# Merging the convolution branch last: two branch merges taken out of the attention's filler steps, and fewer filler steps per turn

## The chip, the cores and the metric

The kernel runs on one core of a Trainium2 chip. The metric is device time in microseconds (us) for one execution of the whole program. The engines are PE (TensorE, matrix products and transposes), DVE (VectorE), ACT (ScalarE), POOL (GpSimd) and SP (SyncE, which issues most of the DMAs). Each of them works through its own list of instructions strictly in the order in which the list was built; semaphores make one engine wait for another.

## The reference

Two layers of a decoder trunk over 512 tokens of 1024 channels, in f32. In each layer three token mixers read the same normalised input `h`, each is projected to 1024 channels by its own matrix, and the three are added under per-channel gates:

```python
h = rmsnorm(x, norm_mix[layer])
z = h @ w_in[layer]
u_glu, q_nsa, kv_nsa, g_nsa, c_q, c_kv, k_rope, g_merge = jnp.split(z, split_at, axis=-1)
y_conv = conformer_conv(u_glu, ...)          # GLU, 31 taps per channel, layernorm, swish, @ w_branch_conv
y_nsa = nsa_attention(q_nsa, ...) @ w_branch_nsa[layer]
y_mla = mla_attention(c_q, c_kv, ...) @ w_branch_mla[layer]
g_conv, g_attn, g_mla = jnp.split(jax.nn.sigmoid(g_merge), 3, axis=-1)
x = x + (g_conv * y_conv + g_attn * y_nsa + g_mla * y_mla) @ w_out[layer]
```

Cross attention over 256 memory tokens and a gated feed-forward net follow in each layer, and one last norm at the end.

## The kernel before, in words

**Arithmetic.** An f32 operand is held as two fp32r parts, a high and a low one. `hilo` (L90) makes them: ACT copies the high part (L93), DVE subtracts it for the low part (L94). A product of two such operands is three matmuls (`mm3`, L85 to L88). One such triple with 512 columns is called a *step* here. Weights come by DMA into `raw` (2 buffers of 1 MB), and `unit` (L105) splits them into `wh` and `wl` (3 buffers each), one unit for 8 steps.

**One layer's mixers** are built by `mix` (L453). The main line of work there is attention, unit by unit: four heads of the latent attention (MLA), then the sparse attention (NSA) in the order of two groups `g`, in each four query tiles `i` = 3, 2, 1, 0 and for each a compressed unit and the selected and window branches (two units of two heads each for `i` > 1, one of four heads otherwise). A unit has scores on PE (`ps_s`, L1020 and L1021), a biased minimum on DVE (L1025), the exponential on ACT (L1028), a reciprocal and gate product on DVE (L1033, L1034), the scaling on ACT (L1036), transposes on PE (`ps_t`, L1065), the split of the transposed probabilities (`PTh` on ACT, `PTl` on DVE) and the products with the values on PE (`ps_pv`, L1075 and L1076). `ps_s`, `ps_t`, `PTh` and `PTl` have two buffers each, `ps_pv` has one. When a query tile is done, `mixture` (L1082) copies and adds it into `o_nsa` (ACT L1088, DVE L1092), and only then has the next tile's `ps_pv` a bank.

**The filler.** Between the attention's instructions stand steps that do not depend on them. `work` (L1095) is a generator of all of these, in one fixed order: the projections and compressions that NSA needs, the convolution's four channel blocks, and at its end two of the three branch merges. `pump(n)` takes the next n steps from it. The loop over the units calls `pump` once per turn (transpose, scores of a later unit, products):

```python
for now in mix(*args, ready[u]):
    next(scores, None)
    products()
    products = now
    pump(6 if u < 4 else 4 if args[1] > 1 else 3)
```

Here `u < 4` are the MLA heads and `args[1]` is the query tile `i`. After the loop `run(filler)` takes what is left, and the third merge, that of NSA, follows.

**The convolution.** `conv_steps(m)` (L553) takes 16 steps on PE, then one DVE instruction at L567 and 30 at L569 (`ca<-u,vT,ca`, one for each tap, called *taps* here). The taps are given a low priority: the builder places them in DVE's list where it finds room. The layer norm and swish are eight jobs: `conv_stats(t)` transposes one token tile on PE (L878, into a `ps_mm` bank), takes mean and variance on DVE (L881 to L883), a power on POOL (L884), and writes `cn` on DVE (L886), which frees the bank; `conv_swish(m)` transposes back (L896), then ACT and DVE make `cS`.

**A merge** (`merge_steps(b, w, act)`, L916) handles one branch b (0 convolution, 1 NSA, 2 MLA) in 8 blocks of 128 channels. Each block has 8 gate steps, which need only `h` (`hTh`, `hTl`), and 4 steps with the branch's output `act` (`om` for MLA, `op` for the two others); so 96 steps in all. The gate of block m + 1 comes ahead of block m's own 4 steps. Branch 2 starts the sum `acc` (L946), the others add to it (L948, L949), and the last one makes `fin`, the split operand of the output projection. The `ps_mm` tag has 3 banks, shared by gates, blocks and the convolution's jobs.

**What sets the order.** The builder keeps, for each engine, roughly the order in which the code is written, but moves an instruction ahead where what stands before it is not ready by its own reckoning. The list that comes out is fixed; the chip follows it.

Of the kernel before, what the change touches and what calls it, by code (L numbers as in the profile page):

```python
# [21 lines left out]
NT = T // 128  # L22
# [30 lines left out]
def kernel(ctx, tc, x, mem, positions, rel_bias, norm_mix, norm_xattn, norm_mem, norm_ffn, norm_final,  # L53
# [399 lines left out]
    def mix(l, x_src, g_mix, x_now, more_x, spill_x, turns):  # L453
# [356 lines left out]
        o_mla = []  # L810
# [62 lines left out]
        cS = []  # L873
# [42 lines left out]
        def merge_steps(b, w, act):  # L916
            blocks = fm_blocks(W, [Z_M + b * D + 128 * m for m in range(KD)], KD)

            def gate():
                p = bank("mm")  # L920
                yield from fm_steps(p, next(blocks), hx, KD)
                gt = new("gm")
                nc.scalar.activation(gt, p, AF.Tanh, scale=0.5)
                ahead.append(gt)

            ahead = []
            yield from gate()
            for m in range(KD):
                if m + 1 < KD:
                    yield from gate()  # L930
                if m % 4 == 0:
                    raw = load(lambda raw: [(raw.rearrange("p (k c) -> p k c", k=4),
                                             w[:, m * 128:m * 128 + 512].rearrange("(k p) c -> p k c", p=128))])
                    rv = raw.rearrange("p (k c) -> p k c", k=4)
                if m % 2 == 0:
                    c = m % 4 * 128
                    wh, wl = unit(rv[:, :, c:c + 256], (4, 256))
                e = m % 2 * 128
                y = bank("mm")
                for k in range(4):  # L940
                    yield
                    mm3(y, wh[:, k, e:e + 128], wl[:, k, e:e + 128], act[k][0], act[k][1], k == 0, k == 3)
                gt = ahead.pop(0)
                if b == 2:
                    acc.append(new("op", name="acc"))
                    nc.vector.scalar_tensor_tensor(acc[m], gt, 1.0, y, op0=OP.add, op1=OP.mult)  # L946
                    continue
                nc.vector.scalar_tensor_tensor(gt, gt, 1.0, y, op0=OP.add, op1=OP.mult)  # L948
                nc.vector.tensor_tensor(acc[m], acc[m], gt, op=OP.add)  # L949
                if b == 1:  # L950
                    fin.append((new("op", dt=F32R), new("op", dt=F32R)))
                    hilo(fin[m][0], fin[m][1], acc[m], 0.5)

# [141 lines left out]
        def work():  # L1095
# [22 lines left out]
            next(out_v)  # L1118
            done.update(("values", "group 1"))
            yield from third  # L1120
            yield from conv_steps(3)

            jobs = {84 + 3 * t: (conv_stats, t) for t in range(NT)} | {99 + 3 * m: (conv_swish, m) for m in range(4)}
            for n, _ in enumerate(chain(merge_steps(2, w_branch_mla[l], o_mla), merge_steps(0, w_branch_conv[l], cS))):
                if n in jobs:
                    yield
                    job, i = jobs[n]
                    job(i)
                yield


        idle = cycle(("s", "t", "s", "t", "pv"))
# [73 lines left out]
        for u, (_, mix, args) in enumerate(units):  # L1206
            scores = start(u + 2 if u < 3 else u + 3)
            for now in mix(*args, ready[u]):
                next(scores, None)
                products()  # L1210
                products = now
                pump(6 if u < 4 else 4 if args[1] > 1 else 3)
            for _ in scores:
                pump(1)
        products()
# [2 lines left out]


        paced["rate"] = 0.17  # L1220
        run(merge_steps(1, w_branch_nsa[l], split4([o_nsa[0][:, k, :] for k in range(4)])))
        return fin, vT[:, 173:181]

    def raw_halves():
# [570 lines left out]
```

## Time and profile before

| | |
|---|---|
| median of 3 runs | 1900.68 us (1900.39 to 1902.31) |
| the profiled execution | 1901.39 us |
| span of its trace | 1899.7 us |
| PE busy | 1877.8 us, 99% of the span |
| DVE busy | 1509.5 us, 79% |
| ACT busy | 1042.1 us, 55% |

All rows are of the one profiled execution; a place in the program is given by its time in us from the span's start. In layer 0 the sparse attention runs from about 190 to 421, and the last merge from there to about 486; layer 1 repeats this some 937 later. In a row of a group, "x12 | 14.7, 1221 | 8.0 <-ACT wh L93" means 12 instructions, 14.7 us busy, 1221 ns for one, and 8.0 us in which the engine stood idle just before them, most of it until that ACT instruction. A matmul's printed length covers its pipeline; what one costs PE is the distance between two starts.

### The profile page before, as it was taken

What the parts mean: (1) busy time and instruction counts of PE and PEld (TensorE: products, weight loads), DVE (VectorE), ACT (ScalarE), POOL (GpSimd) and SP (SyncE); (2) the same over time, 40 slices, a digit from 0 to 9 for tenths busy, and PEclk for the clock granted to TensorE, in tenths of its full rate; (3) what the DMA queues carried; (4) which work ended last, traced back from release to release, by engine and by line L of the source; (5) the groups of instructions that cost most, each with busy time, mean ns of one, the idle gap of its engine ahead of it and who ended that gap; (6) DMA issues with size and microseconds to landing.
All of it is one profiled execution on the core that took longest, in us unless ns stands there. A gap on an engine that the chain in (4) does not pass through costs nothing.

```text
span 1899.7 us, 29485 instructions
## 1 busy us (share of the span) xinstructions
PE 1877.8 (99%) x10988; PEld 1644.1 (87%) x10988; DVE 1509.5 (79%) x2750; ACT 1042.1 (55%) x1947; POOL 270.1 (14%) x434
## 2 busy tenths in 40 slices
PE   9999999999999999999999999999999999999997
PEld 8887888888887999998888878888888889999986
DVE  7999898764466899898869999986555678998986
ACT  5366557763355645456543765675634465445563
POOL 1211111111122211100022111111112221110000
PEclk9999999999999999999999999999999999999999
DMA  6666554456866666656666675535566766766664
GB/s 187 163 156 180 147 128 128 118 149 155 240 178 163 187 166 185 184 179 199 180 180 163 162 197 128 129 98 144 156 185 165 222 171 157 195 164 170 201 198 151
DMA packets 217644, 318.52 MB, mean 168 GB/s; under 512 B 16352, under 2 KB 153843, under 8 KB 217500
## 3 DMA queue, kind: packets, MB, share of 16 engines
q1 hardware_dynamic: 183404, 216.91, 36.4%
q0 software_dynamic: 31872, 94.39, 24.0%
q10 hardware_dynamic: 2224, 5.33, 0.8%
q8 instruction: 86, 1.41, 0.3%
q14 instruction: 58, 0.48, 0.1%
HBM read 307.13 MB, written 97.54 MB: 213 GB/s over the span
## 4 chain that ended last, share of the span: by engine, by line
PE 89%; DVE 5%; issue 3%; ACT 2%; POOL 1%; DMA 1%; POOLq 0%; DVEq 0%; SPq 0%
PE ps_mm L86 14%; PE ps_mm L88 14%; PE ps_mm L87 14%; PE ps_s L86 3%; PE ps_s L88 3%; PE ps_s L87 3%; PE ps_t L87 2%; PE ps_t L86 2%; PE ps_t L88 2%; PE ps_t L1065 2%; PE ps_mm L1355 1%; PE ps_mm L1356 1%; PE ps_mm L1354 1%; PE ps_pv L86 1%; PE ps_pv L88 1%
## 5 line engine op out<-in xcount | busy, mean ns | idle before, releaser
L93 ACT CAST wh<-raw 128x1024 fp32r<-128x1024 f32 (+3 forms) x419 | 422.3, 1011 | 500.9 <-PE ps_mm L87 125.1
L94 DVE TENSOR_TENSOR wl<-raw,wh 128x1024 fp32r<-128x1024 f32 (+3 forms) x419 | 488.6, 1172 | 221.6 <-ACT wh L93 216.0
L86 PE MATMUL ps_mm<-hTh,wh 128*128 128x512 f32 (+1 forms) x1152 | 415.1, 361 | 0.5 <-DVE kc L94 0.5
L87 PE MATMUL ps_mm<-hTl,wh 128*128 128x512 f32 (+1 forms) x1152 | 411.8, 358 | 0.0
L88 PE MATMUL ps_mm<-hTh,wl 128*128 128x512 f32 (+1 forms) x1152 | 411.2, 357 | 0.5 <-DVE wl L94 0.5
L88 PEld LDWEIGHTS ps_mm<-hTh,wl 128*128 128x128 f32 x1152 | 218.1, 189 | 32.7 <-DVE wl L94 1.3
L86 PEld LDWEIGHTS ps_mm<-hTh,wh 128*128 128x128 f32 x1152 | 218.2, 190 | 29.6 <-issue 1.3
L87 PEld LDWEIGHTS ps_mm<-hTl,wh 128*128 128x128 f32 x1152 | 218.3, 190 | 26.5 <-issue 0.7
L569 DVE SCALAR_TENSOR_TENSOR ca<-u,vT,ca 128x512 f32<-128x512 f32 x240 | 177.5, 747 | 2.9
L448 POOL DMA_DIRECT2D up<-in_w_gate_up_dram x128 | 84.9, 663 | 540.2 <-PE ps_mm L88 388.5
L448 POOL DMA_DIRECT2D down<-in_w_down_dram x132 | 85.3, 646 | 480.5 <-PE ps_mm L88 250.7
L93 ACT CAST PTh<-ps_t 128x512 fp32r<-128x512 f32 (+4 forms) x136 | 70.5, 519 | 55.1 <-PE ps_t L1065 40.9
L1028 ACT ACTIVATE P<-P,ss 128x512 f32<-128x512 f32 (+3 forms) x128 | 71.6, 560 | 48.5 <-DVE ss L1025 47.5
L86 PE MATMUL ps_s<-rh,wh 128*128 128x256 f32 x320 | 90.6, 283 | 0.0
L87 PE MATMUL ps_s<-rl,wh 128*128 128x256 f32 x320 | 90.6, 283 | 0.0
L88 PE MATMUL ps_s<-rh,wl 128*128 128x256 f32 x320 | 90.6, 283 | 0.0
L94 DVE TENSOR_TENSOR PTl<-ps_t,PTh 128x512 fp32r<-128x512 f32 (+2 forms) x120 | 71.6, 598 | 9.0 <-ACT PTh L93 7.9
L1036 ACT ACTIVATE P<-P,sr 128x512 f32<-128x512 f32 (+3 forms) x128 | 63.2, 555 | 16.6 <-DVE sr L1034 16.4
L86 PE MATMUL ps_mm<-op,wh 128*128 128x512 f32 (+1 forms) x192 | 68.8, 359 | 0.0
L88 PE MATMUL ps_mm<-op,wl 128*128 128x512 f32 (+1 forms) x192 | 68.4, 356 | 0.3
L87 PE MATMUL ps_mm<-op,wh 128*128 128x512 f32 (+1 forms) x192 | 68.1, 355 | 0.0
L86 PEld LDWEIGHTS ps_s<-rh,wh 128*128 128x128 f32 x320 | 61.4, 192 | 0.0
(555 smaller groups left out, 4646.2 us busy)
## 6 DMA issues: line engine op xcount, KB each, us to landing
up<-in_w_gate_up_dram POOLq DMA_DIRECT2D x128, 320.0 KB, 4.4
down<-in_w_down_dram POOLq DMA_DIRECT2D x132, 256.0 KB, 4.1
raw<-in_w_in_dram SPq DMA_DIRECT2D x32, 1024.0 KB
raw<-in_w_gate_up_dram SPq DMA_DIRECT2D x60, 512.0 KB
raw<-up SPq DMA_DIRECT2D x40, 512.0 KB
raw<-down SPq DMA_DIRECT2D x40, 512.0 KB
raw<-in_w_down_dram SPq DMA_DIRECT2D x30, 512.0 KB
raw<-in_w_in_dram SPq DMA_DIRECT2D x26, 512.0 KB
```

The costliest lines, as they stand in the source:

```text
L86: nc.tensor.matmul(o, lh, rh, start=start, stop=False)
L87: nc.tensor.matmul(o, lh, rl, start=False, stop=False)
L88: tick(nc.tensor.matmul(o, ll, rh, start=False, stop=stop))
L93: nc.scalar.copy(hi, src)
L94: nc.vector.tensor_tensor(lo, src, f(hi), op=OP.subtract)
L448: d = nc.gpsimd.dma_start(dst, src, accum_op=op) if op else nc.gpsimd.dma_start(dst, src)
L569: nc.vector.scalar_tensor_tensor(c, u[:, j:j + T], cw[:, m, j:j + 1], c, op0=OP.mult, op1=OP.add)
L1028: nc.scalar.activation(p[:, c], p[:, c], AF.Exp, bias=s[:, k:k + 1], scale=-1.0, accum_out=s[:, 4 + k:5 + k])
L1036: nc.scalar.activation(P[k], P[k], AF.Copy, scale=r[:, k:k + 1])
L1065: nc.tensor.transpose(tp[:, w:w + 128], P[k][:, j * 128:(j + 1) * 128], ident)
L1354: nc.tensor.matmul(accs[t], xh, u[0][:, k, :], start=j == 0, stop=False)
L1355: nc.tensor.matmul(accs[t], xh, u[1][:, k, :], start=False, stop=False)
```

## The change

The merges change places. The MLA merge stays a filler, but is put ahead of the convolution's last channel block. The convolution's merge and its eight jobs leave the filler: they now come after the attention and behind the NSA merge, in the same order and with the same distances in steps as before (jobs at steps 84 to 108 of the two merges taken together). The filler is 96 merge steps and 8 job places shorter, and a turn takes 3 or 2 steps in place of 4 or 3. `fin` is made in branch 0, the last one now. No instruction is added or removed.

```diff
-                if b == 1:
+                if b == 0:
                     fin.append((new("op", dt=F32R), new("op", dt=F32R)))
                     hilo(fin[m][0], fin[m][1], acc[m], 0.5)
...
             yield from third
+            yield from merge_steps(2, w_branch_mla[l], o_mla)
             yield from conv_steps(3)
-
-            jobs = {84 + 3 * t: (conv_stats, t) for t in range(NT)} | {99 + 3 * m: (conv_swish, m) for m in range(4)}
-            for n, _ in enumerate(chain(merge_steps(2, w_branch_mla[l], o_mla), merge_steps(0, w_branch_conv[l], cS))):
-                if n in jobs:
-                    yield
-                    job, i = jobs[n]
-                    job(i)
-                yield
...
-                pump(6 if u < 4 else 4 if args[1] > 1 else 3)
+                pump(6 if u < 4 else 3 if args[1] > 1 else 2)
...
         paced["rate"] = 0.17
-        run(merge_steps(1, w_branch_nsa[l], split4([o_nsa[0][:, k, :] for k in range(4)])))
+        jobs = {84 + 3 * t: (conv_stats, t) for t in range(NT)} | {99 + 3 * m: (conv_swish, m) for m in range(4)}
+        for n, _ in enumerate(chain(merge_steps(1, w_branch_nsa[l], split4([o_nsa[0][:, k, :] for k in range(4)])),
+                                    merge_steps(0, w_branch_conv[l], cS))):
+            if n in jobs:
+                job, i = jobs[n]
+                job(i)
         return fin, vT[:, 173:181]
```

**PE in layer 0, in the query tile i = 1 of group 1.** Each row is one instruction: line, operation, what it writes and reads (with buffer numbers), size. Before, a turn's transposes (L1065) and products (L1075, L1076) are followed by three steps of the convolution's merge:

```order
L1065 MATMUL ps_t_4429<-ident_81,P_4256 128x128 x2
L1065 MATMUL ps_t_4429<-ident_81,P_4284 128x128 x2
L1075 MATMUL ps_pv_4337<-PTh_4381,V_306 128x512
L1076 MATMUL ps_pv_4337<-PTl_4382,V_306 128x512
L86 MATMUL ps_mm_4428<-op_3518,wh_4424 128x512
L87 MATMUL ps_mm_4428<-op_3519,wh_4424 128x512
L88 MATMUL ps_mm_4428<-op_3518,wl_4425 128x512
L86 MATMUL ps_mm_4428<-op_3560,wh_4424 128x512
L87 MATMUL ps_mm_4428<-op_3561,wh_4424 128x512
L88 MATMUL ps_mm_4428<-op_3560,wl_4425 128x512
```

In the changed kernel the same tile reads, on PE:

```order
L1020 MATMUL ps_s_3913<-op_1443,op_2060 128x128
L1021 MATMUL ps_s_3913<-op_1444,op_2060 128x128
L1075 MATMUL ps_pv_3889<-PTh_3866,V_306 128x512
L1020 MATMUL ps_s_3961<-op_1564,op_1950 128x128
L1021 MATMUL ps_s_3961<-op_1565,op_1950 128x128
L1020 MATMUL ps_s_3961<-op_1564,op_1953 128x128
L1076 MATMUL ps_pv_3889<-PTl_3867,V_306 128x512
L1075 MATMUL ps_pv_3889<-PTh_3896,V_307 128x512
L1021 MATMUL ps_s_3961<-op_1565,op_1953 128x128
L1065 MATMUL ps_t_3902<-ident_81,P_3830 128x128
L1020 MATMUL ps_s_3961<-op_1564,op_2057 128x128
```

The filler has run out by then: its last steps stand in the tile i = 3 of group 1. From there to the attention's end (the tiles i = 2, 1 and 0 of group 1) the only steps in PE's list are ones that were moved ahead from the NSA merge: 24 gate steps, and two of its first block that need group 0's output alone. Before, 78 steps stand in that stretch.

**DVE in layer 0, around the attention's end.** Before, the last products' split (`PTl`), the mixture (L1092) and the split of `o_nsa` for the NSA merge (`op<-o_nsa,op`) stand together, with rows of the convolution's merge (L948, L949) ahead:

```order
L1092 TENSOR_TENSOR o_nsa<-ps_pv,oh 64x2x128
L948 SCALAR_TENSOR_TENSOR gm<-gm,ps_mm 128x512
L651 MEMSET vc 128x256
L949 TENSOR_TENSOR acc<-acc,gm 128x512
L94 TENSOR_TENSOR PTl<-ps_t,PTh 128x512 x2
L94 TENSOR_TENSOR wl<-raw,wh 128x1024
L1092 TENSOR_TENSOR o_nsa<-ps_pv,oh 64x2x128 x2
L94 TENSOR_TENSOR op<-o_nsa,op 128x512 x2
```

In the changed kernel taps of the last channel block (L569) stand among them:

```order
L651 MEMSET vc 128x256
L569 SCALAR_TENSOR_TENSOR ca<-u,vT,ca 128x512 x3
L94 TENSOR_TENSOR PTl<-ps_t,PTh 128x512
L569 SCALAR_TENSOR_TENSOR ca<-u,vT,ca 128x512 x2
L94 TENSOR_TENSOR wl<-raw,wh 128x1024
L1092 TENSOR_TENSOR o_nsa<-ps_pv,oh 64x2x128 x2
L569 SCALAR_TENSOR_TENSOR ca<-u,vT,ca 128x512
L94 TENSOR_TENSOR op<-o_nsa,op 128x512
```

Between the first scores of tile i = 2 of group 1 and the last row of `op<-o_nsa,op`, DVE's list now holds the block's L567 and 18 of its 30 taps, and 4 rows of `wl`; before it held no tap there.

**PE in layer 0, at a `conv_stats` job.** Before, steps of the MLA merge (`om`) and attention scores (L1020, L1021) stand around the transposes:

```order
L1020 MATMUL ps_s_3440<-op_1443,op_1953 128x512
L1021 MATMUL ps_s_3440<-op_1444,op_1953 128x512
L86 MATMUL ps_mm_3401<-om_2050,wh_3335 128x512
L87 MATMUL ps_mm_3401<-om_2051,wh_3335 128x512
L878 MATMUL ps_mm_3424<-ident_81,ca_502 128x128
L878 MATMUL ps_mm_3424<-ident_81,ca_1302 128x128
```

In the changed kernel there are only steps of the NSA merge (`op`):

```order
L88 MATMUL ps_mm_4471<-op_4019,wl_4439 128x512
L86 MATMUL ps_mm_4471<-op_4023,wh_4438 128x512
L87 MATMUL ps_mm_4471<-op_4024,wh_4438 128x512
L878 MATMUL ps_mm_4475<-ident_81,ca_502 128x128
L878 MATMUL ps_mm_4475<-ident_81,ca_1302 128x128
```

From the first job's transposes to the first `conv_swish` transpose PE now has 15 steps and nothing else.

## The prediction

> **What bounds the kernel now.** I read the page first: span, busy times, and the chain that ended last.
>
> ```profile
> span 1899.7 us, 29485 instructions
> PE 1877.8 (99%) x10988; PEld 1644.1 (87%) x10988; DVE 1509.5 (79%) x2750; ACT 1042.1 (55%) x1947; POOL 270.1 (14%) x434
> PE 89%; DVE 5%; issue 3%; ACT 2%; POOL 1%; DMA 1%; POOLq 0%; DVEq 0%; SPq 0%
> ```
>
> PE is the bound, and all the idle time it has is 1899.7 - 1877.8 = 21.9 us. The change neither adds nor removes a PE instruction, so it can save only such idle time. Next, the waits of PE in the stretch that the change touches, 185 to 430 in layer 0 and 1120 to 1370 in layer 1; each answer has one row:
>
> ```profile
> PE ps_mm L878 <- DVE cn L886: 1.3, 1, 1.3
> PE ps_mm L878 <- DVE cn L886: 0.6, 1, 0.6
> ```
>
> In each layer a `conv_stats` job waits once for a bank, together 1.9 us. That is nearly all there is to win: 0.1% of the time. Then the busy time by stretches (columns: stretch, its length, and for PE, weight load, DVE, ACT and POOL the busy us with the number of instructions, then clock and DMA):
>
> ```profile
> 240.00:260.00 20.00, 20.00 (x105) 17.02 (x104) 19.71 (x43) 11.48 (x23) 3.16 (x5) 1.00 0.58 164
> 260.00:280.00 20.00, 20.00 (x112) 17.24 (x111) 19.69 (x44) 10.53 (x22) 2.04 (x4) 1.00 0.49 119
> 346.00:422.00 76.00, 76.00 (x409) 64.44 (x407) 52.24 (x141) 49.27 (x115) 10.26 (x18) 1.00 0.56 152
> ```
>
> While the taps run (240 to 280) DVE is 98% busy, and PE still never waits, because filler steps cover it. At the end of the attention, 346 to 422, DVE is busy 52.24 of 76 us, and PE is again full. This last stretch holds the three query tiles that lose their filler, so the forecast is made there.
>
> **The filler-less end of the attention: the main term.** First PE. Its rows for the steps in 346 to 422, and the starts of one step's matmuls and the next's:
>
> ```profile
> L86 PE MATMUL ps_mm<-hTh,wh 128*128 128x512 f32 x50 | 19.7, 393 | 0.0
> L86 PE MATMUL ps_mm<-op,wh 128*128 128x512 f32 x28 | 11.1, 398 | 0.0
> ...
> 355.94 0.39 PE L86 MATMUL ps_mm<-hTh,wh 128*128 128x512 f32 x1
> 356.62 0.39 PE L86 MATMUL ps_mm<-hTh,wh 128*128 128x512 f32 x1
> ```
>
> A step costs 356.62 - 355.94 = 0.68 us, and 78 of them 53.0; so the attention's own PE work in the stretch is 76.0 - 53.0 = 23.0 us. The changed list has 26 steps there (24 gates and two block steps moved ahead): 17.7 + 23.0 = 40.7 us of PE work.
>
> Now DVE over the same work. The groups that change, in 346 to 422, and the tap's own row from 200 to 300:
>
> ```profile
> L94 DVE TENSOR_TENSOR wl<-raw,wh 128x1024 fp32r<-128x1024 f32 x12 | 14.7, 1221 | 8.0 <-ACT wh L93 7.9
> L94 DVE TENSOR_TENSOR PTl<-ps_t,PTh 128x512 fp32r<-128x512 f32 x13 | 8.8, 686 | 2.6 <-ACT PTh L93 2.6
> L948 DVE SCALAR_TENSOR_TENSOR gm<-gm,ps_mm 128x512 f32<-128x512 f32 x7 | 4.8, 687 | 2.0 <-PE ps_mm L88 1.7
> L949 DVE TENSOR_TENSOR acc<-acc,gm 128x512 f32<-128x512 f32 x7 | 4.8, 683 | 0.1
> L1033 DVE RECIPROCAL sr<-ss 128x4 f32<-128x4 f32 x4 | 0.7, 176 | 2.0 <-ACT P L1028 1.9
> L1033 DVE RECIPROCAL sr<-ss 128x2 f32<-128x2 f32 x4 | 0.7, 164 | 2.3 <-ACT P L1028 2.3
> ...
> L569 DVE SCALAR_TENSOR_TENSOR ca<-u,vT,ca 128x512 f32<-128x512 f32 x60 | 43.9, 749 | 0.5
> ```
>
> From 52.24 go the merge's rows (4.8 + 4.8) and 8 of the 12 weight splits (14.7 x 8 / 12 = 9.8): 32.8 us. To it come the 18 taps and L567, which I cost as one more tap: 19 x 43.9 / 60 = 13.9. DVE has **46.7 us** to do where PE has 40.7. ACT has 49.27 less seven weight casts and three gates:
>
> ```profile
> L93 ACT CAST wh<-raw 128x1024 fp32r<-128x1024 f32 x10 | 10.5, 1050 | 6.5 <-PE ps_mm L87 6.5
> L923 ACT ACTIVATE gm<-ps_mm 128x512 f32<-128x512 f32 x6 | 3.5, 584 | 0.0
> ```
>
> That is 49.27 - 7.35 - 1.75 = 40.2 us, as much as PE. So three engines would each have to be full, in a loop in which each waits for the others: PE for `PTl`, DVE for the exponential, ACT for the scores and for the gate product. The taps stand in DVE's list ahead of splits for which PE waits, and the chip cannot pass them. What is queued behind a waiting PE instruction is all of PE's list, the moved steps too.
>
> The cost per layer has these ends. With DVE never idle, PE loses 46.7 - 40.7 = 6.0 us; the edges of the stretch are good to about 2 us, so 4 at least. At the other end stands the only place where PE starved on DVE's splits for long, around 160 in layer 0, where DVE's own share fell:
>
> ```profile
> 160.00:170.00 10.00, 8.92 (x37) 7.08 (x38) 8.05 (x18) 5.90 (x14) 0.52 (x1) 0.83 0.34 107
> ```
>
> At a share of 0.805, 46.7 us of work take 58.0, and PE loses 17. Between them I take DVE's own waits for ACT in the present stretch, 2.0 + 2.3 before L1033 and 2.6 before `PTl`: 6.9 us, of which the taps fill some; half of it left makes 46.7 + 3.4 - 40.7 = 9.4. I take **9 us a layer, 18 in all**.
>
> **The filled part of the attention** keeps 3 (or 2) steps a turn. The taps that before made DVE 98% busy at 240 to 280 are fewer there now, since 18 of them went to the end; PE's cover, two or three steps (1.4 to 2.0 us) beside the scores and products, still stands against the split of one turn, one cast and one `PTl` (0.69). I cost it at nothing; its ends are nothing, and one wait of 0.4 us a layer as the smaller ones in this trace. A step less in each turn takes away exactly that cover, and where it fails the loss shows as short waits for `PTl`.
>
> **The convolution's jobs** now stand between steps of the NSA merge alone. The 1.9 us of waits go with their old place. What is late next is DVE's part of a job; its rows from 300 to 325, and from the timeline the first job's transposes and its `cn`, then the fourth job with the wait:
>
> ```profile
> L886 DVE TENSOR_SCALAR cn<-ps_mm,mv 128x512 f32<-128x512 f32 x4 | 3.2, 805 | 0.8 <-POOL mv L884 0.7
> L881 DVE BATCH_NORM_STATS2 bn<-ps_mm 128x6 f32<-128x512 f32 x4 | 2.8, 695 | 0.0
> ...
> 303.25 0.60 PE L878 MATMUL ps_mm<-ident,ca 128*128 128x128 f32 x4
> ...
> 307.02 0.81 DVE L886 TENSOR_SCALAR cn<-ps_mm,mv 128x512 f32<-128x512 f32 x1
> ...
> 318.07 0.63 PE L878 MATMUL ps_mm<-ident,ca 128*128 128x128 f32 x4 [1.27 <-DVE cn L886]
> ```
>
> A bank was held for 307.02 + 0.81 - 303.25 = 4.6 us. Now the next jobs come after three or four steps (2.0 to 2.7 us) with three banks in turn, and `cn` of the fourth job is wanted 5 steps (3.4 us) later. From the first job to the first swish PE has 15 steps and 16 transposes, about 12 us; DVE has four jobs at some 1.8 us (0.70 and 0.81 of these rows, and two small ones), two pairs L948 and L949 and two weight splits, 7.3 + 2.7 + 2.4 = 12.4. So the loss lies between 0.4 and what one late `cn` costs for a job, 3 us; by the row it is nearest to, the 1.27 above, I take 1.1 a layer. That gives back what was won: -1.9 + 2.2 = +0.3.
>
> **Costed at nothing.** The MLA merge ahead of the last channel block: the same steps in another order. `fin` in branch 0 instead of 1: L94 and L93 rows of the same sizes at the same distance from the output projection. SP: every weight load moves with its steps, two buffers ahead as before, and the transfers' share in 346 to 422 is 0.56. POOL: the paced transfers go by a count of steps, which stays. If the cover of one of these fails it is a single wait, 0.2 to 0.6 us by the waits of this trace.
>
> **A rule that bears on the main term.** Where PE waited around 160, its clock fell right after (columns as above; the clock is the third value from the end):
>
> ```profile
> 158.00:162.40 4.40, 2.60 (x10) 1.28 (x9) 4.24 (x10) 2.99 (x8) 0.01 (x1) 1.00 0.77 244
> 162.40:165.90 3.50, 3.50 (x10) 2.71 (x9) 3.28 (x9) 2.38 (x7) 0.52 (x1) 0.51 0.27 59
> ...
> 160.64 0.50 PE L863 MATMUL ps_pv<-PTl,op 128*128 128x512 f32 x1 [1.18 <-DVE PTl L94]
> ...
> 163.23 0.63 PE L86 MATMUL ps_mm<-hTh,wh 128*128 128x512 f32 x1
> 163.66 0.63 PE L87 MATMUL ps_mm<-hTl,wh 128*128 128x512 f32 x1
> ```
>
> A matmul then took 0.43 us (163.66 - 163.23) in place of 0.23 for 3.4 us, a loss of about 1.6. The longest wait before it was 1.18 us. The same place of layer 1 shows no fall:
>
> ```profile
> 1100.00:1120.00 20.00, 18.82 (x105) 15.87 (x106) 19.09 (x41) 13.01 (x31) 2.10 (x3) 1.00 0.63 169
> ```
>
> The Trainium skill, "TensorE: Matmul & The Clock Gate", section "Why this matters for your kernels", says that only an idle gap of more than about 3 us drops the clock to half. By that rule short waits leave the sum as it is; by the row a crowd of waits of about 1 us can be enough, and that is the second rival.
>
> **The rivals.** (1) *The filler is enough.* The moved steps fill every hole and the builder's order suits the chip: PE stays full at the end, the old waits go, and the jobs run free. For it speaks that PE has no idle time at 240 to 280 with DVE 98% busy; against it, that DVE then was not in PE's loop, and that its 46.7 us do not fit into 40.7. It decides if DVE's work in the stretch comes to under 41 us. Time: 1901.4 - 1.9 = 1899.5 with nothing lost, 1904.5 with some: not slower. (2) *The clock falls in the filler-less end.* If three windows of 3.4 us a layer run at half clock, 2 x 3 x 1.6 = 9.6 come on top: about 1929. For it, the fall at 162; against it, the clock at 1100 under the same waits, and that a slow PE also waits less. (3) *The cost falls on the filled part*, where a turn has a step less, and not on the end: waits for `PTl` then spread over 190 to 300, a few tenths in each of some 25 turns, 2 x 25 x 0.3 = 15 us: about 1916, hard to tell by the time alone.
>
> **How the numbers follow.** The sum is made on the profiled execution: 1901.39 + 18 + 0.3 = 1919.7. That execution lies 0.7 above the median of the runs shown, so I predict **1919**. Chances: the forecast, 1906 to 1932, 0.68; rival 1 0.13; rival 2 0.12; rival 3 0.05; 0.02 for more than 0.2% faster, which the 1.9 us to win and a clock fall that stays away (1.6) do not reach. The low end is 4 us a layer less the 1.9: 1900.7 + 8 - 1.9 = 1906.8; the high end 17 a layer and 2.2 for the jobs: 1937. I give **1906 to 1936**. A measurement of this kernel can tell 0.2%, 3.8 us, from no change; so faster 0.02, same 0.12, slower 0.86.
>
> **What would show it.** In the changed profile, PE's waits from about 300 to 360 in layer 0 (and 937 later) should add up to 7 to 11 us, most of them before `ps_pv` and `ps_t` and until DVE `PTl`, and DVE should be over 90% busy there with 18 taps among them. PE's wait at L878 should be under 2 us a layer. Before 300 there should be next to none. It is wrong if PE is full through that end (rival 1), if the granted clock falls there (rival 2), or if the waits lie before it (rival 3); and if the end loses far more than 11 us a layer, the half of the ACT waits that I left in was too little.

## The result, and the profile after

| | before | changed |
|---|---|---|
| median of 4 runs | 1901.49 us (1900.39 to 1902.58) | 1918.10 us (1917.29 to 1918.81) |
| the profiled execution, its span | 1901.39, 1899.7 us | 1918.81, 1917.1 us |

The changed kernel takes 1.0085 times as long (95% interval 1.0073 to 1.0097). The forecast of 1919 us holds for the time. It does not hold for the place, nor for what makes PE wait there.

The changed kernel's page (span, busy time, chain that ended last):

```profile
span 1917.1 us, 29558 instructions
PE 1886.3 (98%) x10988; PEld 1645.8 (86%) x10988; DVE 1514.5 (79%) x2750; ACT 1039.9 (54%) x1947; POOL 271.3 (14%) x434
PE 84%; DVE 6%; ACT 4%; issue 3%; DMA 1%; POOL 1%; SPq 0%; POOLq 0%; DVEq 0%; ACTq 0%
```

The span grew by 17.4 us, PE's idle time only from 21.9 to 1917.1 - 1886.3 = 30.8. The other 8.5 us count as PE busy, with the same 10988 matmuls: one that is not followed at once is printed longer (0.50 us at 1322.33 in the last section, 0.39 in a full stretch), and at half clock longer still (0.63 at 1323.50). Such a loss is read from the distances between starts.

From a layer's first compressed score (L980) to its first output-projection matmul (L1252, in the kernel before L1254) the kernel before takes 296.9 us in layer 0 and 295.5 in layer 1, the changed one 304.8 and 304.5: **7.9 and 9.0 us more**, nearly all of the 17.4. Here are PE's waits in that stretch, all that are listed, layer 0 (300 to 440), then layer 1 (1250 to 1385):

```profile
PE ps_mm L86 <- ACT op L93: 2.0, 1, 2.0
PE ps_pv L1075 <- ACT PTh L93: 1.1, 2, 0.9
PE ps_t L1065 <- ACT P L1036: 1.0, 3, 0.5
PE ps_t L1421 <- ACT hn L214: 0.6, 1, 0.6
PE ps_mm L878 <- DVE mv L883: 0.3, 1, 0.3
PE ps_mm L896 <- DVE cn L886: 0.3, 1, 0.3
...
PE ps_mm L86 <- ACT op L93: 1.5, 1, 1.5
PE ps_t L1065 <- ACT P L1036: 0.9, 2, 0.7
PE ps_pv L1075 <- ACT PTh L93: 0.9, 1, 0.9
PE ps_mm L87 <- DVE op L94: 0.5, 1, 0.5
PE ps_mm L896 <- DVE cn L886: 0.3, 1, 0.3
```

The largest wait lies behind the attention: the NSA merge's first steps (L86, L87) wait for the split of `o_nsa`. No wait for `PTl` is listed. By stretches (columns as in the prediction), the tiles i = 2 and 1 of group 1 together, then the last tile, i = 0. A tile is counted here from its first compressed score (L980), the last one to the last product; the last products of the tile ahead still fall into it:

```profile
322.58:352.07 29.49, 29.45 (x188) 25.78 (x186) 25.45 (x82) 23.65 (x57) 3.29 (x7) 1.00 0.28 70
352.07:371.79 19.72, 18.41 (x101) 14.89 (x99) 18.27 (x61) 16.72 (x53) 1.83 (x3) 1.00 0.43 124
```

In the first two of the three tiles that lost their filler PE is full. The end of the third, in the changed kernel's timeline: PE's last product and what follows, then what ACT and DVE do between:

```profile
371.79 0.39 PE L1076 MATMUL ps_pv<-PTl,V 128*128 128x512 f32 x1
...
373.15 0.39 PE L88 MATMUL ps_mm<-op,wl 128*128 128x512 f32 x1
375.54 0.73 PE L86 MATMUL ps_mm<-op,wh 128*128 128x512 f32 x2 [2.00 <-ACT op L93]
...
371.76 1.06 ACT L93 CAST wh<-raw 128x1024 fp32r<-128x1024 f32 x1 [1.90 <-PE ps_mm L87]
372.84 0.58 ACT L1088 COPY oh<-ps_pv 64x512 f32<-64x512 f32 x1
374.87 0.62 ACT L93 CAST op<-o_nsa 128x512 fp32r<-128x512 f32 x1 [1.44 <-DVE o_nsa L1092]
...
372.85 1.22 DVE L94 TENSOR_TENSOR wl<-raw,wh 128x1024 fp32r<-128x1024 f32 x1
373.99 0.84 DVE L1092 TENSOR_TENSOR o_nsa<-ps_pv,oh 64x256 f32<-64x256 f32 x2
```

From the last product to the first step that needs it (375.54 - 371.79) 3.75 us pass: copy, sum, cast, with a weight unit's cast and split ahead of the copy and the sum. PE had two steps left for that. The kernel before had the same way, but gate steps without a gap over it:

```profile
421.61 0.39 PE L1076 MATMUL ps_pv<-PTl,V 128*128 128x512 f32 x1
...
424.33 0.39 PE L87 MATMUL ps_mm<-hTl,wh 128*128 128x512 f32 x1
...
424.18 1.30 DVE L94 TENSOR_TENSOR op<-o_nsa,op 128x512 fp32r<-128x512 f32 x2 [0.69 <-ACT op L93]
```

The loss by place, in us for layer 0 / layer 1. I worked it out from the trace: the time of a stretch, less what its PE instructions take by the median start-to-start distance of their kind in the kernel before (so a full stretch can come out slightly below zero).

| | tile i = 3 of group 1 | tiles i = 2 and 1 | last tile, i = 0 | behind the last product, to L1252 |
|---|---|---|---|---|
| before | 1.6 / 0.9 | -0.1 / -0.1 | 0.0 / 0.0 | -0.2 / -0.1 |
| changed | 1.2 / 1.4 | 0.5 / 0.5 | 2.5 / 2.1 | 5.0 / 5.7 |

So over half of the loss lies behind the attention. Of it some 2.5 us a layer are the wait for the split with the refilling of PE's pipeline; 1.0 and 0.8 the convolution's jobs; 0.8 in layer 0 transposes of the memory's norm (L1421) that wait for ACT; and about 1.6 in layer 1 a fall of the clock (the last section). The rest, 0.7 and 0.8, I did not place.

The last tile's loss stands at its beginning: 2.1 of 2.5 us in layer 0 and 1.8 of 2.1 in layer 1 lie ahead of the last product of tile i = 1 (363.14 and 1308.61), while that tile's last units pass through ACT. The largest piece, 1.0 us by the distance of starts, on PE and then on ACT:

```profile
353.90 0.49 PE L1065 MATMUL ps_t<-ident,P 128*128 128x128 f32 x3
...
356.31 0.50 PE L1075 MATMUL ps_pv<-PTh,V 128*128 128x512 f32 x1 [0.86 <-ACT PTh L93]
...
355.06 0.49 ACT L1028 ACTIVATE P<-P,ss 128x256 f32<-128x256 f32 x1
...
355.68 1.07 ACT L93 CAST PTh<-ps_t 128x512 fp32r<-128x512 f32 x2
```

The transposes are done at 354.39, but their casts stand in ACT's list behind four exponentials (from 353.58), and ACT has no gap from 351.98 to 356.75. Of this loss at least, ACT's queue is the cause.

### The profile page after: what moved, and what is told of

It is laid out like the page before. It is cut to its first block, busy times and chain, and to the rows that moved or that the text cites. A ratio compares the mean times of both kernels' runs of the same rounds, so it can differ in the third digit from the quotient of the medians.

```text
span 1917.1 us, 29558 instructions
## 1 busy us (share of the span) xinstructions
PE 1886.3 (98%) x10988; PEld 1645.8 (86%) x10988; DVE 1514.5 (79%) x2750; ACT 1039.9 (54%) x1947; POOL 271.3 (14%) x434
## 4 chain that ended last, share of the span: by engine, by line
PE 84%; DVE 6%; ACT 4%; issue 3%; DMA 1%; POOL 1%; SPq 0%; POOLq 0%; DVEq 0%; ACTq 0%
PE ps_mm L86 14%; PE ps_mm L87 14%; PE ps_mm L88 14%; PE ps_s L86 3%; PE ps_s L88 3%; PE ps_s L87 2%; PE ps_t L86 2%; PE ps_t L87 2%; PE ps_t L88 2%; PE ps_t L1065 2%; PE ps_mm L1353 1%; PE ps_mm L1354 1%; PE ps_mm L1352 1%; PE ps_pv L86 1%; PE ps_pv L88 1%
## 5 line engine op out<-in xcount | busy, mean ns | idle before, releaser
L86 PE MATMUL ps_mm<-hTh,wh 128*128 128x512 f32 (+1 forms) x1152 | 415.8, 361 | 0.5 <-DVE kc L94 0.5
L87 PE MATMUL ps_mm<-hTl,wh 128*128 128x512 f32 (+1 forms) x1152 | 411.6, 358 | 0.0
L86 PEld LDWEIGHTS ps_mm<-hTh,wh 128*128 128x128 f32 x1152 | 218.4, 190 | 30.3 <-issue 1.3
L87 PEld LDWEIGHTS ps_mm<-hTl,wh 128*128 128x128 f32 x1152 | 218.3, 190 | 26.9 <-issue 0.7
L569 DVE SCALAR_TENSOR_TENSOR ca<-u,vT,ca 128x512 f32<-128x512 f32 x240 | 179.3, 747 | 3.7
L86 PE MATMUL ps_s<-rh,wh 128*128 128x256 f32 x320 | 90.6, 283 | 0.0
L87 PE MATMUL ps_s<-rl,wh 128*128 128x256 f32 x320 | 90.6, 283 | 0.0
L86 PE MATMUL ps_mm<-op,wh 128*128 128x512 f32 (+1 forms) x192 | 68.7, 360 | 3.5 <-ACT op L93 3.5
L87 PE MATMUL ps_mm<-op,wh 128*128 128x512 f32 (+1 forms) x192 | 69.4, 362 | 0.5 <-DVE op L94 0.5
L1036 ACT ACTIVATE P<-P,sr 128x512 f32<-128x512 f32 (+3 forms) x128 | 63.1, 553 | 11.2 <-DVE sr L1034 10.4
L86 PEld LDWEIGHTS ps_s<-rh,wh 128*128 128x128 f32 x320 | 61.4, 192 | 0.0
```

The source lines that it names most:

```text
L86: nc.tensor.matmul(o, lh, rh, start=start, stop=False)
L87: nc.tensor.matmul(o, lh, rl, start=False, stop=False)
L569: nc.vector.scalar_tensor_tensor(c, u[:, j:j + T], cw[:, m, j:j + 1], c, op0=OP.mult, op1=OP.add)
L1036: nc.scalar.activation(P[k], P[k], AF.Copy, scale=r[:, k:k + 1])
```

## The experiments

"+" is how much longer the way from L980 to L1252 is than before, layer 0 / 1. "Steps" are those in PE's list in the tiles i = 2, 1, 0 of group 1 of layer 0. The losses, worked out as above, are for layer 0; a dash where the kernel's other lines make them not comparable. One fall of the clock ahead of the attention (at about 162 or 1104, some 1.6 us) comes and goes between kernels: before and changed have it at 162, e5 also at 1104, e4 and e9 not at all. "+" leaves it out.

| kernel | median us | ratio to before, 95% | + | steps | loss in last tile, behind it |
|---|---|---|---|---|---|
| before | 1901.49 | 1 | 0 / 0 | 39, 20, 22 | 0.0, -0.2 |
| changed | 1918.10 | 1.0085 (1.0073 to 1.0097) | 7.9 / 9.0 | 13, 6, 12 | 2.5, 5.0 |
| e1 rate 4 or 3 | 1933.28 | 1.0169 (1.0155 to 1.0183) | 16.4 / 16.7 | 13, 6, 1 | 9.1, 7.2 |
| e2 rate 2 or 1 | 1912.67 | 1.0058 (1.0046 to 1.0071) | 4.8 / 5.7 | 21, 11, 16 | 2.1, 1.6 |
| e3 block earlier | 1910.93 | 1.0050 (1.0038 to 1.0063) | 4.1 / 4.6 | 11, 3, 9 | 2.4, 1.5 |
| e4 no taps | 1908.68 | 1.0044 (1.0030 to 1.0058) | 4.2 / 4.5 | 12, 2, 10 | 2.3, 1.5 |
| e5 before, rate 3 or 2 | 1907.55 | 1.0029 (1.0018 to 1.0040) | 1.9 / 2.5 | 24, 15, 19 | 1.5, -0.1 |
| e6 gate held | 1926.23 | 1.0126 (1.0113 to 1.0140) | 11.2 / 12.6 | 13, 6, 4 | - |
| e7 block behind | 1912.79 | 1.0058 (1.0046 to 1.0071) | 4.9 / 5.3 | 9, 3, 17 | 2.2, 1.8 |
| e8 11 taps | 1916.68 | 1.0081 (1.0068 to 1.0094) | 8.8 / 7.6 | 13, 6, 12 | 2.5, 5.7 |
| e9 casts on DVE | 1911.65 | 1.0050 (1.0037 to 1.0064) | 4.2 / 4.9 | 12, 3, 8 | 2.5, 1.5 |
| e10 held and 11 taps | 1924.11 | 1.0123 (1.0107 to 1.0138) | 10.3 / 11.0 | 13, 6, 4 | - |
| e11 block earlier, 2 or 1 | 1912.90 | 1.0057 (1.0044 to 1.0069) | 3.9 / 4.3 | 21, 10, 15 | 2.1, 1.6 |
| c1 before, jobs spread | 1905.69 | 1.0022 (1.0012 to 1.0031) | 1.7 / 2.1 | as before | 0.0, -0.2 |

### Which part of the change costs: rate, merges, block order

**e5** is the kernel before with the changed rate alone.

```diff
-                pump(6 if u < 4 else 4 if args[1] > 1 else 3)
+                pump(6 if u < 4 else 3 if args[1] > 1 else 2)
```

> The kernel before, with the changed kernel's 3 or 2 filler steps a turn and nothing else changed. The filler then lasts beyond the attention, which keeps 66 steps and jobs in its last three tiles (before: 81, the changed kernel: 31), and the filled tiles ahead have as many steps as in the changed kernel. Shortage at the end: nothing is lost, 1899 to 1904 us. Filled part: the 17 us come with the rate alone, 1914 to 1920 us.

It cost 5.7 us (1907.55 against 1901.87 in the same comparison), between the two. Not in waits over the filled tiles, though: 1.5 us of a layer's loss lie in the last tile, the rest in single waits in the tiles i = 2 and 1.

**e3** is the changed kernel with the last channel block ahead of the MLA merge again.

```diff
-            yield from merge_steps(2, w_branch_mla[l], o_mla)
             yield from conv_steps(3)
+            yield from merge_steps(2, w_branch_mla[l], o_mla)
```

> The changed kernel with the last channel block ahead of the MLA merge again, as in the kernel before; all else as changed. Its taps are then done in the tile i = 3 of group 1, none is left in the last three tiles, and PE's list has 23 steps there (the changed kernel: 31). Theory of the taps: what cost 8 to 9 us a layer was DVE's 46.7 us of work in those tiles, 13.9 of them taps; without them DVE has about 32 against PE's 23.0 + 23 x 0.68 = 38.6, and next to nothing is lost: 1900 to 1906 us. Theory of the loop: DVE's taps only fill time that DVE has; the pace comes from the way from scores over minimum, exponential, scaling, transposes and casts back to PE, with ACT's 40 us on it, and with fewer steps PE waits longer: 8 steps fewer at 0.68 are 5.4 us more loss a layer, 1920 to 1932 us.

1910.9: again between. Put in a row, the rate alone costs 5.7 us, the convolution's merge and jobs behind the attention 3.4 more, and the block order, which the prediction took for "the same steps in another order", the last 7. By "+", both layers together, these are 4.4, 4.3 and 8.2. The shares hold for this order of steps only: with the merges moved, the lower rate does not cost but saves (e1).

**e1** is the changed kernel with the old rate, and **e2** with a lower one:

```diff
-                pump(6 if u < 4 else 3 if args[1] > 1 else 2)
+                pump(6 if u < 4 else 4 if args[1] > 1 else 3)   # e1
+                pump(6 if u < 4 else 2 if args[1] > 1 else 1)   # e2
```

> The changed kernel with the 4 or 3 filler steps a turn of before: the moved merges alone, without the lower rate. The filler then runs out in the tile i = 3 of group 1; PE's list has 14, 13, 6 and 1 steps in the last four query tiles (the changed kernel: 25, 13, 6, 12), and DVE's has 3, 7, 3 and 12 taps there. Theory of the sum: in the last four tiles PE has 22 steps fewer than in the changed kernel, 15 us a layer that DVE and ACT, with 7 taps more, do not get shorter by: 1935 us or more. Theory of the handover and the last tile: only the tile i = 0 and the way behind it lose; with one step in it the last tile loses some 3 us more, and the tile i = 3 one or two: 1920 to 1930 us. If the lower rate were what costs, it would be faster than the changed kernel: 1905 to 1912 us.

> The changed kernel with 2 or 1 filler steps a turn in place of 3 or 2, so that the filler lasts through the attention: PE's list then holds 48 steps in the last three query tiles (the changed kernel: 31, before: 81 with the convolution's jobs), and 37, 21, 10, 7 and 18 in the five tiles ahead of them (42, 30, 15, 12, 25); 8 taps stand in the last three tiles (18). Two theories of the 17 us. Shortage at the end: PE has too few steps only in the last three tiles. With 48 steps PE has 23.0 + 48 x 0.68 = 55.6 us of work there against some 42 of DVE, so no wait is left there, and the five tiles ahead stay full: 1899 to 1905 us. Filled part: a step fewer per turn costs a short wait in every turn, wherever it stands; then this kernel, with two steps fewer than before in some 25 turns a layer, loses more than the changed one: 1925 us or more.

Both came out between their theories. e1 lost 31 us: with the moved merges the lower rate is needed. PE's waits of e1 in layer 0 (300 to 440), the two largest:

```profile
PE ps_pv L1052 <- ACT P L1036: 3.3, 1, 3.3
PE ps_mm L86 <- ACT op L93: 2.2, 1, 2.2
```

In e1 the tiles i = 2 and 1 still lose nothing with 19 steps; the last tile with one step loses 9.1 and the way behind it 7.2. Part of that is the clock: it stood at half for 3.4 us from 364.8 and for 10.2 from 375.0, and in layer 1 for 13.7 from 1327.3. e2's filler lasts through the end, and it gains 5 us; but the last tile still loses 2.1, with 16 steps in it, and the tile i = 0 of group 0 a new 1.9.

### Is it DVE's taps?

**e4** leaves the last block's 30 taps out.

```diff
-            for j in range(1, TAPS):
+            for j in range(1, TAPS if m < 3 else 1):
```

> The changed kernel without the 30 taps of the last channel block (L569 for m = 3; its first product at L567 stays), in both layers. DVE's list has no tap then from the tile i = 1 of group 0 on, and PE's 24 steps in the last three tiles. Theory of the taps: 1900 to 1906 us, with PE's waits in the last three tiles under 2 us a layer. Theory of the loop: PE waits as before for ACT's casts and scalings, 8 us a layer or more since there are 7 steps fewer: 1917 to 1930 us. The wait for the split of the output behind the last query tile (2.0 us in layer 0 and 1.5 in layer 1 of the changed kernel) stays by both.

1908.7: near the theory of the taps, though not in its range. But the builder also made another list for PE. Here is the gate's first matmul in the tiles i = 2 and 1 of the changed kernel, then of e4, then the two tiles' busy times in e4:

```profile
L86 PE MATMUL ps_mm<-hTh,wh 128*128 128x512 f32 x19 | 7.5, 397 | 0.0
```

```profile
L86 PE MATMUL ps_mm<-hTh,wh 128*128 128x512 f32 x14 | 5.5, 393 | 0.0
```

```profile
320.88:347.32 26.44, 26.40 (x174) 23.56 (x173) 20.58 (x75) 22.05 (x54) 3.29 (x7) 1.00 0.31 78
```

With 14 steps PE is as full there as with 19. So the five others covered nothing, and made these tiles 29.49 - 26.44 = 3.1 us longer. In e4 they stand behind the last product: the NSA merge's first step starts 4.07 us after it, without a wait.

```profile
364.99 0.39 PE L1076 MATMUL ps_pv<-PTl,V 128*128 128x512 f32 x1
...
368.84 0.39 PE L87 MATMUL ps_mm<-hTl,wh 128*128 128x512 f32 x1
369.06 0.39 PE L86 MATMUL ps_mm<-op,wh 128*128 128x512 f32 x1
```

**e8** tells the two apart. It keeps 11 of the 30 taps and leaves 19 out (the first words on record have this the wrong way round; what follows "that is" is the edit). PE's list stays that of the changed kernel.

```diff
-            for j in range(1, TAPS):
+            for j in range(1, TAPS if m < 3 else 12):
```

> The changed kernel with 11 of the last channel block's 30 taps left out in full order, that is with the taps 1 to 11 kept and 12 to 30 left out, in both layers. PE's list is that of the changed kernel step for step; in DVE's list 7 taps are missing in the last query tile (4 in place of 11) and the rest behind the attention. Theory that DVE sets the end: from the first scores of tile i = 2 of group 1 to the split output the changed kernel takes 54.9 and 54.5 us, with 49.4 of PE work in it; 7 x 0.75 = 5.2 us less on DVE shorten it to 50 to 51, by 4 us a layer: 1909 to 1912 us. Theory that ACT or the way through the engines sets it and the taps only fill holes: unchanged, 1916 to 1919 us.

1916.7, unchanged within the intervals. The last tile of e8:

```profile
352.16:371.90 19.74, 18.45 (x101) 14.88 (x99) 16.00 (x57) 16.73 (x52) 1.83 (x3) 1.00 0.44 124
```

DVE has 2.3 us less to do than in the changed kernel (16.00 against 18.27; three of the taps left out had run inside this tile), the tile takes 19.74 us instead of 19.72, and the wait of 2.0 before L86 stays. DVE's time on these taps is not what PE waits for. The taps left out had all stood behind 368 us, though, not where the tile loses its 2.1 us; for that part e3 and e4 speak, which have no tap there and still lose 1.8 and 1.7. So what e4 gained came, as far as these runs tell, with PE's other list.

### Is it ACT?

**e9** is e3 with the NSA merge's weights cast on DVE (in `unit`, for gates and branch of b = 1).

```diff
-        hilo(hv, lv, src)
+        if dve:
+            nc.vector.tensor_copy(hv, src)
+            nc.vector.tensor_tensor(lv, src, f(hv), op=OP.subtract)
+        else:
+            hilo(hv, lv, src)
```

> The kernel with the last channel block ahead of the MLA merge (23 steps and no taps in the last three query tiles, 1910.9 us), with the high parts of the NSA merge's weights, gates and branch alike, cast on DVE in place of ACT. PE's list has 23 steps in the last three tiles again; ACT has three casts of 1.05 us less there, DVE three copies more. There ACT was busy 17.43 of 17.58 us in the last tile, DVE 13.48. Theory that ACT sets the end once the taps are away: the last tile falls from 17.6 towards the 15.2 of PE's own work, 2 us a layer: 1906 to 1908 us. Theory that the way through all the engines sets it: unchanged or, with more on DVE, slower: 1910 to 1914 us.

The last tile in e3, then in e9:

```profile
348.49:366.07 17.58, 16.78 (x91) 12.97 (x90) 13.48 (x51) 17.43 (x54) 2.04 (x4) 1.00 0.22 42
```

```profile
347.43:363.99 16.56, 15.40 (x86) 12.26 (x85) 13.71 (x53) 15.80 (x51) 1.32 (x2) 1.00 0.19 41
```

The tile got 1.0 us shorter in layer 0 and 0.2 in layer 1, with a step less in it in layer 0. PE loses as much there as before (2.5), and the time is the same, 1911.65. So the weight casts are not what PE waits for. Whether the rest of ACT's work is, e9 cannot tell: in e3 ACT's weight casts start at 347.19 and 365.44, and 1.8 of the 2.4 us that PE loses in this tile lie before 359.49, with no such cast to take away.

### Where the last steps stand

**e6** is the changed kernel with the third NSA gate kept behind the last product (its lines from L921 on are numbered 5 to 6 higher).

```diff
+                if b == 1 and m == 2:
+                    with tc.issue_after(latest["v"].ins):
+                        yield from steps
```

> The changed kernel with one edge more: the 8 steps of the third gate of the NSA merge may not be placed ahead of the attention's last product. In the changed kernel the builder put all 24 gate steps that it could move ahead of that product, and nothing is left behind it to cover the way from the last product over the copy, the sum and the split of the output to the merge's first steps (waits of 2.0 us in layer 0 and 1.5 and 0.5 in layer 1 before L86 and L87). DVE's list stays as it is, with all its 18 taps; PE's list has 4 steps in the last query tile in place of 12, and 8 behind it. Theory of the handover: these waits are a matter of place; 8 x 0.68 = 5.4 us of steps cover 3.7 us of chain, and the last tile does not lose what is won: 1912 to 1915 us. Theory of the sum: DVE's (and ACT's) work in the last three tiles sets when the output is ready, wherever PE's steps stand; what the handover wins the last tile loses: 1916 to 1920 us.

1926.2, worse than by either theory. The wait for the split is gone, but the last product came no sooner, although PE had 8 steps fewer ahead of it. PE in e6: the last product of tile i = 1, the first and the last of tile i = 0:

```profile
361.41 0.49 PE L1081 MATMUL ps_pv<-PTl,V 128*128 128x512 f32 x1
...
365.95 0.77 PE L1057 MATMUL ps_pv<-PTh,vc 128*128 128x512 f32 x1 [2.76 <-ACT gm L928]
...
369.88 0.80 PE L1081 MATMUL ps_pv<-PTl,V 128*128 128x512 f32 x1
```

and ACT and DVE between them:

```profile
364.15 0.58 ACT L1094 COPY oh<-ps_pv 64x512 f32<-64x512 f32 x1
...
364.96 0.84 DVE L1098 TENSOR_TENSOR o_nsa<-ps_pv,oh 64x256 f32<-64x256 f32 x2
```

`ps_pv` has one bank: the last tile cannot start its sum before the tile ahead is copied and added (365.80 here; the row names the gate's activation, which ended 0.04 later). From the last product of tile i = 1 to that start pass 4.5 us in e6, 4.8 in the changed kernel, 4.2 in e4, 4.7 in e1 and 4.1 in the kernel before. This time goes through ACT and DVE; what differs most is how many steps PE has to put beside it. In the changed kernel there are some six and PE loses 0.3 us; with one (e6) it loses 3.2, with none (e1) 3.6. The length depends on ACT's order. In e2 only 2.3 us pass, because the copy comes as soon as the product is done; in the changed kernel it stands behind four exponentials (e2, then changed):

```profile
354.11 0.58 ACT L1088 COPY oh<-ps_pv 64x512 f32<-64x512 f32 x1 [0.31 <-PE ps_pv L1076]
...
365.90 0.58 ACT L1088 COPY oh<-ps_pv 64x512 f32<-64x512 f32 x1
```

The same way, copy and sum, then stands behind the last product. In about 12 us (363.14 to 375.54 in the changed kernel) PE needs cover twice; it has it the first time and not the second. In e6 its clock fell as well (from 365.7), which lengthened the last piece.

**e10** joins the edits of e6 and e8.

> Both of the last edits at once: the 8 steps of the third gate kept behind the attention's last product, and of the last channel block's 30 taps only the first 11 done, in both layers. PE's list has 4 steps in the last query tile, DVE's 4 taps. Alone, the held gate left the last product where it was (49.1 us behind the first scores of tile i = 2 of group 1, the changed kernel 49.2), and so did the fewer taps (49.3). Theory of two ways of equal length: PE's own list with its waits is one of them, the way over DVE's taps the other, and each held the end while the other was shortened; with both shortened the last product comes 3 to 5 us earlier (without any tap and with 24 steps it was 44.1), and the held gate covers the split: 1909 to 1914 us. Theory of a fixed way through scalings, casts and copies that neither taps nor steps are part of: the last product stays at 49, and the time is that of the held gate alone, 1922 to 1927 us.

1924.1: within the theory of a fixed way. The last product came 48.2 us behind the first score of tile i = 2 in layer 0 (e6: 49.1), 48.6 in layer 1 (48.9).

**e7** puts the last block behind the attention.

```diff
+        run(conv_steps(3))
         jobs = {84 + 3 * t: (conv_stats, t) for t in range(NT)} | {99 + 3 * m: (conv_swish, m) for m in range(4)}
```

> The changed kernel with the last channel block (16 steps, its taps behind them) taken out of the filler and put behind the attention, ahead of the NSA merge; the builder may still pull its steps ahead. PE's list then has 16, 9, 3 and 17 steps in the last four query tiles (the changed kernel: 25, 13, 6, 12), and more steps than the handover needs behind them; 11 taps stand in DVE's list behind the last tile's maximum, none in the two tiles ahead. Theory of the handover: the two tiles i = 2 and 1 lost next to nothing in the changed kernel, and a few steps fewer there matter little; the waits for the split of the output go: 1908 to 1913 us. Theory of the sum: PE has 17 steps fewer before the output is ready than the changed kernel, 11.6 us, against 7 taps fewer (5.1 us) on DVE: 1920 us or more.

1912.8, as the theory of the handover had it: with 17 steps in the last tile and some seven behind the last product the wait for the split is gone. The tiles i = 2 and 1 have only 12 steps, 7 fewer than in the changed kernel, and lose 0.6 us, about as much as there (0.5).

### A better version?

**e11** joins e3 and e2; **c1** tries to take the old waits of the kernel before.

```diff
-            jobs = {84 + 3 * t: (conv_stats, t) for t in range(NT)} | {99 + 3 * m: (conv_swish, m) for m in range(4)}
+            jobs = {78 + 5 * t: (conv_stats, t) for t in range(NT)} | {99 + 3 * m: (conv_swish, m) for m in range(4)}
```

> The kernel with the last channel block ahead of the MLA merge, with 2 or 1 filler steps a turn: the two edits that brought most, together, as the best form of the moved merges. PE's list has 46 steps in the last three query tiles (23 with 3 or 2 a turn), DVE's 13 taps in the first two of them and none in the last, and there are 37, 21, 10, 7 and 18 steps ahead. If the losses of the two add up by place, the end has its cover back (2 us a layer less than with 3 or 2 a turn) and the tile i = 0 of group 0 loses 1.9 a layer as it did with 2 or 1: 1907 to 1911 us. If the thinner filler only moves the loss from the end to the tiles ahead: 1911 to 1914 us. By neither is it as fast as the kernel before.

> The kernel before, with its four conv_stats jobs 5 steps apart from step 78 on in place of 3 apart from step 84 on; nothing else changed. If the waits of PE for a bank there (1.3 us in layer 0, 0.6 in layer 1) come from the jobs' distance, they go: 1899 to 1900.5 us, which a measurement can hardly tell from no change. If they come from DVE's load there, they stay or move to another job: 1900.5 to 1902.5 us.

e11 is no faster than e3: the end still loses 2.1 in the last tile, and the tile i = 0 of group 0 loses 1.7. c1 is slower than before by 0.22%, outside both of its theories. The jobs' waits for a bank did not go, and a wait for a `PTl` came in addition, so it is not their distance alone. That `PTl` stands in DVE's list behind an instruction (L987) that waits for a DMA. PE's waits of c1 in layer 0 (185 to 440), then that row of DVE:

```profile
PE ps_pv L1076 <- DVE PTl L94: 1.6, 1, 1.6
PE ps_mm L878 <- DVE cn L886: 1.3, 2, 0.9
...
313.44 0.25 DVE L987 TENSOR_TENSOR Pc<-ps_s,BT 128x62 f32<-128x62 f32 x1 [1.88 <-DMA BT<-vd]
```

No version beat the kernel before.

## Why the prediction was right and where it failed

- **The bound.** Right: PE is the bound, there was nothing to win beyond the 1.9 us of waits, and idle PE time made the loss.
- **The main term, 9 us a layer.** Measured 7.9 and 9.0, but the step behind it failed. It set DVE's work over the tiles i = 2, 1, 0 (46.7 us) against PE's (40.7) and let the fuller engine set the end. Here is the stretch that answers to 346 to 422, from 4.3 us behind the first score of tile i = 2 to the last product:

```profile
326.90:371.79 44.89, 43.54 (x259) 36.82 (x257) 41.16 (x131) 37.70 (x103) 4.34 (x9) 1.00 0.28 75
```

DVE did 41.2 us of work in it, and PE 42.0, the 44.9 less the 2.9 that it lost. DVE was not the fuller engine; two of the 18 taps and a weight split, 2.7 us, came only behind the last product. The forecast wanted 7 to 11 us of waits from 300 to 360, mostly until `PTl`; from 300 to the last product about 2 us are listed, all until ACT, and in the tiles i = 2 and 1 PE lost 0.5 us. With less work on DVE (e8) nothing changed. What the runs show in its place are two losses: in the last tile 2.5 and 2.1 us, nearly all at its beginning, in waits for ACT's scalings and casts; and behind it the way from the last product over copy, sum and cast to the split, 3.75 us with two steps beside it. The sum came out right by luck, because two errors met: too much in the tiles, nothing behind them.
- **What the forecast left out** is the way behind the last product. It counted 26 steps moved ahead as cover and did not ask what was left for the split of `o_nsa`: 5.0 and 5.7 us a layer are lost there. That too few steps stood there is shown: in e2, e3, e4 and e7, with more of them, the loss behind the last product is 1.3 to 1.8 in both layers.
- **"Costed at nothing": block order.** Wrong: it is worth 7 us (e3), by the builder's placing of gate steps where PE was full anyway. That the taps in DVE's list are what led the builder to it is argued from e4 and e8, not shown.
- **The filled part.** Right for the changed kernel: before 300 PE has one wait of 0.2 us in layer 0, two of 0.3 in layer 1. Yet e5 shows that the rate alone costs 5.7 us, most of it in the last three tiles.
- **The jobs.** The +2.2 was right in size: their waits now cost 1.0 and 0.8 us, about half of it at L878. The old waits went, but nothing was won where they had been: the tile i = 3 of group 1 loses 1.2 and 1.4 us in place of 1.6 and 0.9, now in waits of its transposes for ACT.
- **The rivals.** (1) The filler was not enough. (2) The clock fell, but in one window in layer 1 and none in layer 0, about 1.6 us in place of 9.6. (3) No crowd of `PTl` waits over the filled part.

Open is how far the loss falls if gate steps are held back from the tiles i = 2 and 1, not from the last tile as e6 did; that was not tried. Nor is it settled what the last tile's loss, 1.5 us or more in every kernel with a thin filler, would be with another order on ACT: the trace shows 1.0 us of it as a queue there, and no run changed that order.

## What to carry to other kernels

Count filler where it is needed, not in total: find the places where only one dependent way is left (the handover of a single bank, the handover to the next stage), time that way, and keep that many independent steps for exactly there. Steps that a scheduler spends in a stretch that is full anyway are lost for the end. A high busy share of another engine does not say that it sets the pace: take work away from it with the other engines' order unchanged, and in the very place where the wait is.

## What the hardware showed unexpectedly

The clock fell to half after waits well under 2 us. PE in the changed kernel, layer 1, and the window by its clock:

```profile
1321.12 0.73 PE L86 MATMUL ps_mm<-op,wh 128*128 128x512 f32 x2 [1.46 <-ACT op L93]
1322.33 0.50 PE L87 MATMUL ps_mm<-op,wh 128*128 128x512 f32 x1 [0.47 <-DVE op L94]
...
1323.50 0.63 PE L88 MATMUL ps_mm<-op,wl 128*128 128x512 f32 x1
1323.92 0.63 PE L86 MATMUL ps_mm<-op,wh 128*128 128x512 f32 x1
```

```profile
1323.20:1326.60 3.40, 3.40 (x9) 2.29 (x8) 1.99 (x4) 0.73 (x1) 0.82 (x2) 0.50 0.80 299
```

A matmul takes 0.42 us there in place of 0.23, for 3.4 us. In layer 0 of the same execution a single wait of 2.00 us was followed by no fall. In e8 it was the other way round: the wait of 2.0 us is there in both layers, and the clock fell in layer 0 (from 377.1) and not in layer 1. So neither the longest wait nor the place decides it alone. The Trainium skill, "TensorE: Matmul & The Clock Gate", section "Why this matters for your kernels", names idle gaps of more than about 3 us as what makes the clock fall back; this trace differs, since no gap near the fall in layer 1 reached 2 us.

A wait also costs more than its printed length: at 373.15 the wait of 2.00 us made the distance to the next start 375.54 - 373.15 = 2.39 in place of 0.23, a loss of 2.16.
